# Hybrid decoder trunk on one Trainium2 core: the head norms' widening copy moved ahead of a wait, waits of the side jobs changed, the embedding gate's tanhs issued together

## The chip, the core and the metric

The kernel runs on one core of one Trainium2 chip. The metric is the device time of one execution in microseconds (us), from the first to the last instruction with what the launch adds around them. Engines are named as the profile names them: PE is TensorE (PEld its weight loads), DVE VectorE, ACT ScalarE, POOL GpSimd, SP SyncE, which here does nothing but issue the transfers of weights and small tables from HBM.

## The reference, cut to what matters

256 tokens of width 1024 go through two layers. In each, one projection `w_in` of the normed tokens feeds four mixers (SSD, native sparse attention or NSA, RWKV-7, sliding-window attention or SWA), whose gated outputs are summed and added to the tokens; then comes a feed-forward part (dense in layer 0, two of eight experts in layer 1) and a gated per-layer embedding:

```
x = x + W_o( sum_m sigmoid(gate_m(h)) * (mixer_m(u_m) @ P_m) )
x = x + FFN(RMSNorm(x))
x = x + sigmoid(x @ W_pg) * (p[i] @ W_pp)
# inside RWKV-7, H = 8 heads of N = 64:
kk = (k * k_k).reshape(B, S, H, N)
kk = kk / max(sqrt(sum(kk * kk, -1)), 1e-12)          # head norm 1
o  = (o - mean) * rsqrt(var + RWKV_GN_EPS)            # head norm 2, also over 64
o  = o + sum(r * k * r_k, -1) * v                     # "bonus"
```

The SWA mixer rotates its queries and keys by the tokens' positions (rope), with tables of cosines and sines over 256 positions.

## The kernel before, in words

**Units.** All products with weights go through one list of units, one panel of 128 x 1024 (or 128 x 832) weights each. A unit of kind `fm` is 24 matmuls of 128x256, three for each of eight slices of the width; one of kind `tokm` has 12 or 24 wider ones. Every fp32 product is three matmuls (`mm3`, L357 to L359): high part by high part, low by high, high by low.

**A unit's way.** SP fetches the panel (`raw`, L264) into one of four buffers. ACT copies the high part `H` (L313), and the low part `L = raw - H` is made by DVE for the first three quarters of the columns (L316) and by POOL for the rest (L318). There are three pairs of `H` and `L`. A raw buffer comes free when all three engines have read it, and SP issues its transfers in order. PE needs `H` and the DVE part of `L` from the unit's first slices on, and POOL's quarter only in its later slices.

**Side jobs.** The mixers' other work (norms, scans, attention) is written as generators, which run between pieces of the units: each piece calls `tick()`, which takes 0.64 off the time that every job has left, and a job whose time is up emits its instructions up to the next `yield`. The number after `yield` gives the wait, rounded up to whole ticks, unless the table `WAITS` names another number of ticks for this yield of this job. So the table sets how many of the units' matmuls stand on PE between an instruction of a side job and the one that depends on it. In an `fm` unit one tick is six matmuls. Every engine takes its instructions strictly in the emitted order. When a unit needs a flag of a side job, ticks go by without units until the flag is set.

**The jobs that matter here.** `rwkv_half` runs four times (two halves of the heads in each layer; `rwkv_half0` and `1` are layer 0). For each head norm it calls `head_rsqrt`: four tiny matmuls sum the squares per head (`ssp`, L708), DVE takes a reciprocal root in small steps (`rsqrt_steps`, the last writes `ssc`, L412), and then the job waits 1.8, which is three ticks. After that `head_spread` widens the 8 columns `ssc` to 512 (`wide`, a DVE copy, L717), and PE transposes `wide` (`spr`, L721) so that DVE can multiply by it (`kkn`, L765, or `cen`, L913). Later in the job DVE makes `bq` (L787), and PE sums it over the heads (`bop`, L792), then come `gram` (L818) and `tok` (L800) products. The last step of a half sets a flag that the first NSA unit (`open_pool`) needs. The job `swa` takes the projected queries from ACT (`rraw`, L1363) and PE rotates them (`rotp`, L1380); DVE, POOL and ACT make the rotated, split query of it (`rtmp`, `qTH`).

**Rope tables.** In layer 0 a job issues a transfer of the positions on SP (`pos`, L391), and POOL converts them and reduces the angles in ten instructions (L520 to L530). They stand in POOL's order between two quarters of weight panels.

**Embedding.** `ple_units` handles the gate's columns in two halves. For each of two token tiles ACT takes a tanh (`th`, L1619), DVE adds and multiplies (L1620 on), and squares for the next norm follow.

Of the kernel before, what the change touches and what calls it, by code (L numbers as in the profile page):

```python
# [15 lines left out]
ALU = mybir.AluOpType  # L16
# [32 lines left out]
def _consts():  # L49
# [37 lines left out]
    for k, v in cols.items():  # L87
# [27 lines left out]
}  # L115


def trunk_kernel(tc, I, out, dbg=None, upto=99):
    nc = tc.nc
# [24 lines left out]
    x = big.tile([P, 2, D], F32, name="x")  # L144
# [25 lines left out]
    def K(name):  # L170
        o, w = COFF[name]
        return cst[:, o:o + w] if o < NC32 else cstb[:, o - NC32:o - NC32 + w]
# [16 lines left out]
    def psb(name="psb"):  # L189
        return psB.tile([P, 512], F32, tag="b", name=name)  # L190
# [7 lines left out]
    def unit(run, pieces=None, nk=0, ncol=0, need=None, spawn=None, rich=None, ahead=True, lend=False):  # L198
        stream.append((run, pieces, nk, ncol, need, spawn, rich, ahead, lend))
# [18 lines left out]
    def tick(t=0.64):  # L218

        for g in list(side):  # L220
            g[1] -= t
            if g[1] > 1e-3:
                continue
            if len(g) == 2:
                nm = g[0].gi_code.co_name
                c = spawned[nm] = spawned.get(nm, -1) + 1
                g += [nm + str(c), 0]
                w = wait_of(g, 0)
                if w > 1e-3:
                    g[1] = w - t  # L230
                    if g[1] > 1e-3:
                        continue
            try:
                d = next(g[0])
                if d == "poll":
                    g[1] = 0.3
                else:
                    g[3] += 1
                    g[1] = wait_of(g, d or 1.2)
            except StopIteration:  # L240
                side.remove(g)
# [172 lines left out]
    def rsqrt_steps(t):  # L414
        w = 2 if t.free_size() == 1 else 3
        for n, _ in enumerate(rsqrt_ops(t)):
            if n in (2, 2 + w, 2 + 2 * w):
                yield 0.64
# [5 lines left out]
    def squares(i, n):  # L424

        act(junk, x[:, i, n * 512:n * 512 + 512], AF.Square, accum_out=ssq[:, n, i:i + 1])  # L426
        if n == 0:
            ts(ssq[:, 0, i:i + 1], ssq[:, 0, i:i + 1], 1.0 / D, EPS, ALU.mult, ALU.add)
# [76 lines left out]
    def cols_of(src, c0, w):  # L505
        r = src.rearrange("(k p) n -> p k n", p=P)
        return lambda v, k0, nk: [(v, r[:, k0:k0 + nk, c0:c0 + w])]
# [32 lines left out]
    gfin = []  # L540
# [6 lines left out]
    def mixing(l, after):  # L547
# [105 lines left out]
        def R(name):  # L653
            return Z.mxr.tile([P, 512], F32, tag="r2", name=name, bufs=R2)
# [48 lines left out]
        def head_rsqrt(sq, c, op):  # L703

            ps = psb("ssp")
            bo = K("bo")[:, 0:P:64]
            for n in range(4):
                mm(ps[:, 2 * n:2 * n + 2], sq[:, n * P:(n + 1) * P], bo, start=True, stop=True)  # L708
            ss = Z.mxr.tile([P, 4, 2], F32, tag="ssc", name="ssc", bufs=2)
            ts(ss, ps[:, 0:8].rearrange("p (n h) -> p n h", h=2), c, None, op)  # L710
            yield from rsqrt_steps(ss)
            yield 1.8
            return ss

        def head_spread(ss):
            wide = R("wide")
            vec.tensor_copy(wide.rearrange("p (n v) -> p n v", v=64),  # L717
                            ss.rearrange("p n h -> p (n h)").unsqueeze(2).to_broadcast([P, 8, 64]))
            ps = psb("spr")
            for n in range(4):  # L720
                nc.tensor.transpose(ps[:, n * P:(n + 1) * P], wide[:, n * P:(n + 1) * P], ident)  # L721
            return ps
# [855 lines left out]
    def ple_units(l, Z):  # L1578
        unit(lambda: l + 1 in early and early[l + 1]())

        def settle():
            while side:
                tick()
            rich_close(f"ffn{l}")

        unit(settle)
        if Z.before is not None:
            unit(Z.before)

        def begin():  # L1590
            Z.late = Z.ctx.enter_context(tc.tile_pool(name=f"late{l}", bufs=1))
            rich_open(f"ple{l}", 2, 3)
            if last and upto >= 20:
                for i in range(2):
                    for n in range(2):
                        fin[i, n] = Z.late.tile([P, 512], F32, tag=f"fin{i}{n}", name="fin")
            if Z.after is None:
                Z.xT = to_T(x, 8, big, "hT", name="xT")
                return
            steps = []  # L1600
            Z.xT = to_T(x, 8, big, "hT", name="xT", steps=steps)
            Z.after()
            steps.pop(0)()
            steps.pop(0)()

            def rest():
                for f in steps:
                    f()
                    yield 0.64
                flags.add(f"xT{l}")  # L1610
            side.append([rest(), 0.0])

        unit(begin)
        last = l + 1 == DEPTH
        fin = {}

        def add(i, n, ps):
            th = Z.late.tile([P, 512], F32, tag="th", name="th", bufs=2)
            act(th, ps, AF.Tanh, scale=0.5)  # L1619
            stt(th, th, 1.0, Z.pj[:, i, n * 512:n * 512 + 512], ALU.add, ALU.mult)  # L1620
            o = x[:, i, n * 512:n * 512 + 512]
            stt(o, th, 0.5, o, ALU.mult, ALU.add)  # L1622
            squares(i, n)
            if last and upto >= 20:
                nc.gpsimd.tensor_tensor(fin[i, n], o, gfin[n], ALU.mult)

        def first_half(psl):
            for i in range(2):
                add(i, 0, psl[i])

        def second_half(i, ps):
            add(i, 1, ps)
            if not last and i:
                rms((0, 1), True)
            if last and upto >= 20:
                rms((i,), False)
                for n in range(2):
                    o, r = fin[i, n], rs[0][:, i:i + 1]
                    if n or i == 0:
                        ts(o, o, r, None, ALU.mult)  # L1640
                    else:
                        act(o, o, AF.Copy, scale=r)  # L1642
                    nc.sync.dma_start(out[0, i * P:(i + 1) * P, n * 512:n * 512 + 512], o)

        for n in range(2):
            tok_matmul(lambda: Z.xT, 8, 512, cols_of(I["ple_gate"][l], n * 512, 512), second_half if n else first_half,
                       rich=f"ple{l}", by_token=n == 1, half_need=[f"xT{l}"] if Z.after is not None and n == 0 else None)
        unit(lambda: rich_close(f"ple{l}"))
        unit(Z.ctx.close)
# [55 lines left out]
    def rich_open(key, nraw, nspl):  # L1705

        c = ExitStack()
        r = c.enter_context(tc.tile_pool(name="r" + key, bufs=nraw))
        w = c.enter_context(tc.tile_pool(name="w" + key, bufs=nspl))
        rich[key] = Slots(r, nraw, w, nspl)  # L1710
        rich[key].close = c.close

    def rich_close(key):
        rich.pop(key).close()
# [254 lines left out]
    for l in range(DEPTH):  # L1969
        if upto <= 10 * l:  # L1970
            break
        Z = SimpleNamespace(ctx=ExitStack(), GT={}, OHT={}, rc={}, before=None, after=None)
        mixing(l, (lambda l=l, Z=Z: ffn_open(l, Z), lambda Z=Z: ple_turn(Z),
                   lambda n, l=l, Z=Z: (moe_settled if l % 2 else dense_settled)(l, Z, n)))
        dump_x(f"xmix{l}")
        if upto <= 10 * l + 1:
            break
        (moe if l % 2 else dense)(l, Z)
# [29 lines left out]
```

## Time and profile before

| what | value |
|---|---|
| median of three timed runs | 2025.96 us (2024.52 to 2027.46) |
| the profiled execution | 2029.14 us, span of its instructions 2027.3 us |
| busy: PE / DVE / ACT / POOL | 1941.3 / 1535.2 / 1176.2 / 1108.8 us |
| mean granted TensorE clock | 0.987 of full speed |

PE is busy for 96% of the span, so a reader looks for its idle stretches and for stretches in which its clock is not full. All durations in the rows below come from the profiled execution, and times of day are us from its first instruction. A row of the timeline with `[3.30 <-DVE wide L717]` says that the engine stood idle for 3.30 us just before, and that the DVE instruction of line 717 ended the wait.

### The profile page before, as it was taken

The page shows a single profiled execution, that of the slowest core. Times are in us where ns is not written, and L with a number is a line of the kernel's source. Part 1 is how long each engine was busy: PE and PEld are TensorE (multiplying, and loading weights), DVE is VectorE, ACT ScalarE, POOL GpSimd, SP SyncE. Part 2 cuts the span into 40 slices and gives each one's busy share as a digit, 9 for nine tenths or more (in the row PEclk, how much of TensorE's full clock was granted, in tenths as well). Part 3 has the DMA queues.
Part 4 walks back from the last instruction along what each step waited for, and adds up shares of the span by engine and source line. Part 5 has one row for each costly group of instructions (what it writes and reads, how often), then busy time and mean ns, then how long its engine had stood idle before and what let it go on. Part 6 is the DMA issues. An engine that isn't in the chain of part 4 may idle for free. (4 is left out here: it accounts for less than half of the span.)

```text
span 2027.3 us, 37453 instructions
## 1 busy us (share of the span) xinstructions
PE 1941.3 (96%) x13236; PEld 1612.7 (80%) x13236; DVE 1535.2 (76%) x2432; ACT 1176.2 (58%) x1786; POOL 1108.8 (55%) x976
## 2 busy tenths in 40 slices
PE   6999999999999899999999999999999999999996
PEld 6898787778999688878877777787777777877775
DVE  5565656656554656656666589999999999999995
ACT  5434345455444433334454568777877787778773
POOL 4533254555554353424444566676867666768673
PEclk9999999999999999999999999999999999999998
DMA  7322464466665443227344889899999999999972
GB/s 199 96 75 88 106 142 135 125 173 198 190 189 150 120 120 85 86 82 155 107 135 135 283 275 356 306 327 344 358 349 325 344 360 349 325 347 359 347 254 96
DMA packets 419441, 435.78 MB, mean 215 GB/s; under 512 B 67876, under 2 KB 355624, under 8 KB 419240
## 3 DMA queue, kind: packets, MB, share of 16 engines
q1 hardware_dynamic: 419240, 433.26, 68.1%
q8 instruction: 106, 1.74, 0.3%
q14 instruction: 95, 0.78, 0.1%
HBM read 432.13 MB, written 1.05 MB: 214 GB/s over the span
## 5 line engine op out<-in xcount | busy, mean ns | idle before, releaser
L318 POOL TENSOR_TENSOR L<-raw,H 128x256 fp32r<-128x256 f32 (+1 forms) x794 | 941.9, 1195 | 835.5 <-ACT H L313 658.1
L316 DVE TENSOR_TENSOR L<-raw,H 128x768 fp32r<-128x768 f32 (+1 forms) x792 | 935.2, 1210 | 193.4 <-ACT H L313 186.8
L313 ACT CAST H<-raw 128x1024 fp32r<-128x1024 f32 x794 | 828.2, 1047 | 268.0 <-PE tokm L359 60.8
L357 PE MATMUL gu<-H,GH 128*128 128x512 f32 x704 | 286.4, 407 | 0.1
L358 PE MATMUL gu<-L,GH 128*128 128x512 f32 x704 | 278.9, 396 | 0.5 <-DVE L L316 0.5
L359 PE MATMUL gu<-H,GL 128*128 128x512 f32 x704 | 278.2, 395 | 1.1 <-DVE GL L370 1.1
L359 PE MATMUL dn<-H,aL 128*128 128x512 f32 x440 | 174.7, 397 | 1.4 <-DVE aL L367 1.4
L357 PE MATMUL dn<-H,aH 128*128 128x512 f32 x440 | 174.8, 397 | 1.2 <-ACT aH L366 1.0
L358 PE MATMUL dn<-L,aH 128*128 128x512 f32 x440 | 174.9, 398 | 0.0
L357 PE MATMUL fm<-hTH,H 128*128 128x256 f32 x560 | 168.1, 300 | 0.0
L358 PEld LDWEIGHTS gu<-L,GH 128*128 128x128 f32 x704 | 132.6, 188 | 37.3 <-DVE L L316 10.8
L358 PE MATMUL fm<-hTL,H 128*128 128x256 f32 x560 | 159.1, 284 | 0.0
L359 PE MATMUL fm<-hTH,L 128*128 128x256 f32 x560 | 158.9, 284 | 0.0
L359 PEld LDWEIGHTS gu<-H,GL 128*128 128x128 f32 x704 | 132.3, 188 | 30.3 <-DVE GL L370 2.7
L357 PEld LDWEIGHTS gu<-H,GH 128*128 128x128 f32 x704 | 132.3, 188 | 27.1 <-ACT GH L369 0.5
L357 PE MATMUL tokm<-H,hTH 128*128 128x512 f32 (+1 forms) x320 | 136.9, 428 | 0.0
L358 PE MATMUL tokm<-L,hTH 128*128 128x512 f32 (+1 forms) x320 | 125.5, 392 | 0.5 <-DVE L L316 0.5
L359 PE MATMUL tokm<-H,hTL 128*128 128x512 f32 (+1 forms) x320 | 125.6, 392 | 0.0
L357 PEld LDWEIGHTS fm<-hTH,H 128*128 128x128 f32 x560 | 107.6, 192 | 5.7 <-issue 2.7
L358 PEld LDWEIGHTS fm<-hTL,H 128*128 128x128 f32 x560 | 107.7, 192 | 0.3
L359 PEld LDWEIGHTS fm<-hTH,L 128*128 128x128 f32 x560 | 107.6, 192 | 0.0
L358 PEld LDWEIGHTS dn<-L,aH 128*128 128x128 f32 x440 | 82.9, 188 | 23.1 <-DVE L L316 6.3
(500 smaller groups left out, 3518.0 us busy)
## 6 DMA issues: line engine op xcount, KB each, us to landing
raw<-moe_w_gate SPq DMA_DIRECT2D x341, 256.0 KB
raw<-moe_w_up SPq DMA_DIRECT2D x341, 256.0 KB
raw<-moe_w_down SPq DMA_DIRECT2D x169, 512.0 KB
raw<-w_in SPq DMA_DIRECT2D x126, 512.0 KB
raw<-ffn_w_gate SPq DMA_DIRECT2D x22, 512.0 KB
raw<-ffn_w_up SPq DMA_DIRECT2D x22, 512.0 KB
raw<-ffn_w_down SPq DMA_DIRECT2D x22, 512.0 KB
raw<-w_in SPq DMA_DIRECT2D x32, 256.0 KB
```

The costliest lines, as they stand in the source:

```text
L313: nc.scalar.copy(H[:, :n], raw[:, :n])
L316: tt(L[:, :m], raw[:, :m], H[:, :m], ALU.subtract)
L318: nc.gpsimd.tensor_tensor(L[:, m:n], raw[:, m:n], H[:, m:n], ALU.subtract)
L357: mm(o, l[0], r[0], start=start, stop=False)
L358: mm(o, l[0], r[1], start=False, stop=False)
L359: mm(o, l[1], r[0], start=False, stop=stop)
```

## The change

Three edits. The widening copy is put into `head_rsqrt`, before the wait, and that wait's own default goes from 1.8 to 2.4 (four ticks). `WAITS` gives longer waits: after `ssc` and `wide` of the first norm (yield 6 of each half) 5 or 6 ticks for 2 or 3, between `bq` and the job's next look at its flag (yield 10 of halves 0 and 2) 4 or 5 for 2, after the second norm's copy (yield 43) 4 or 6 for 2 or 3, and before three of the SWA rotations 7 to 9 for 4. In the embedding's first half both tanhs are issued before the additions, and the squares after both.

```diff
-    'rwkv_half0': {1: 7, 3: 2, 6: 2, 12: 1, 15: 3, 18: 2, 20: 5, 22: 2, 23: 4, 24: 2, 28: 7, 29: 1, 31: 4,
-        32: 5, 33: 6, 34: 4, 35: 4, 39: 3, 41: 5, 42: 3, 43: 2, 44: 2},
+    'rwkv_half0': {1: 7, 3: 2, 6: 5, 10: 4, 12: 1, 15: 3, 18: 2, 20: 5, 22: 2, 23: 4, 24: 2, 28: 7, 29: 1, 31: 4,
+        32: 5, 33: 6, 34: 4, 35: 4, 39: 3, 41: 5, 42: 3, 43: 4, 44: 2},
...
-    'swa0': {2: 6, 3: 2, 5: 5, 6: 7, 11: 3, 13: 6, 14: 3},
+    'swa0': {2: 6, 3: 2, 4: 9, 5: 5, 6: 7, 11: 3, 13: 6, 14: 3},
...
             yield from rsqrt_steps(ss)
-            yield 1.8
-            return ss
-
-        def head_spread(ss):
             wide = R("wide")
             vec.tensor_copy(wide.rearrange("p (n v) -> p n v", v=64),
                             ss.rearrange("p n h -> p (n h)").unsqueeze(2).to_broadcast([P, 8, 64]))
+            yield 2.4
+            return wide
+
+        def head_spread(wide):
             ps = psb("spr")
...
         def first_half(psl):
+            ths = [gate(ps) for ps in psl]
             for i in range(2):
-                add(i, 0, psl[i])
+                add(i, 0, ths[i])
+            for i in range(2):
+                settled(i, 0)
```

On DVE, at the first head norm of layer 0, the difference (- before, + after) reads as follows; `r` and `v` are parts of the RWKV projection, `L` the low part of a weight panel.

```order
 L412 SCALAR_TENSOR_TENSOR ssc<-rsa,rsy 128x8
+L713 COPY wide<-ssc 128x512
 L668 SCALAR_TENSOR_TENSOR r<-fm,par,r 128x255
 L316 TENSOR_TENSOR L<-raw,H 128x640
-L717 COPY wide<-ssc 128x512
+L668 SCALAR_TENSOR_TENSOR v<-fm,par,v 128x255
 L765 SCALAR_TENSOR_TENSOR kkn<-k,par,spr 128x256 x2
```

The copy now stands right behind `ssc`. On PE `spr` moves 18 `fm` matmuls back, from 36 behind `ssp` to 54 behind it, so that `kkn` comes after a further projection step on DVE; `bop` moves 15 `tokm` matmuls back.

On PE, in the value units of layer 0 some microseconds later, the rows around the second slice of the third such unit stood like this before (the numbers tell tiles apart; `H_636` and `L_637` are that unit's parts, `kap`, `beta` and `v` belong to the RWKV job).

```order
L358 MATMUL tokm_643<-L_637,hTH_175 128x416
L359 MATMUL tokm_643<-H_636,hTL_176 128x416
L800 MATMUL tok_757<-cst_82,kap_598 64x64 x16
L800 MATMUL tok_776<-cst_82,v_580 64x64 x16
L357 MATMUL tokm_643<-H_636,hTH_175 128x416
L358 MATMUL tokm_643<-L_637,hTH_175 128x416
```

And with the change (the unit's parts are now `H_633` and `L_634`):

```order
L358 MATMUL tokm_640<-L_634,hTH_175 128x416
L359 MATMUL tokm_640<-H_633,hTL_176 128x416
L818 MATMUL gram_705<-AR_598,beta_601 64x128 x8
L357 MATMUL tokm_640<-H_633,hTH_175 128x416
L358 MATMUL tokm_640<-L_634,hTH_175 128x416
L359 MATMUL tokm_640<-H_633,hTL_176 128x416
L800 MATMUL tok_719<-cst_82,beta_601 64x64 x16
L818 MATMUL gram_738<-AR_598,kap_618 64x128 x8
```

Five groups of the RWKV job that stood ahead of this slice (one `tok` of `beta`, two `gram` of `kap`, one `tok` of `kap`, one of `v`) now stand behind it. The slice is the first of its unit that reads POOL's quarter.

On POOL, from the product `kp` of the first RWKV half to the first instruction of the rope tables, the difference is two rows that change places; the quarter of the third value unit still stands behind the ten rope instructions, as before.

```order
 L770 TENSOR_TENSOR kp<-kp,k 128x512
-L776 TENSOR_TENSOR AR<-r,Dd 128x8x64
-L318 TENSOR_TENSOR L<-raw,H 128x192
+L318 TENSOR_TENSOR L<-raw,H 128x192
+L776 TENSOR_TENSOR AR<-r,Dd 128x8x64
 L782 TENSOR_TENSOR kap<-kp,inv 128x512
 L520 CAST scr<-pos 128x256
```

The quarter of the second value unit is now ahead of `AR`. In the emission itself, the second RWKV half of each layer now ends three ticks later, and in each layer three ticks go by without units ahead of `open_pool`, where none did before.

## Rows read from the trace of the kernel before

**Rows 1.** The page's first part: engines, busy us, share, instructions.

```profile
PE 1941.3 (96%) x13236; PEld 1612.7 (80%) x13236; DVE 1535.2 (76%) x2432; ACT 1176.2 (58%) x1786; POOL 1108.8 (55%) x976
```

**Rows 2.** PE's waits, whole span: us in total, times, longest us.

```profile
PE spr L721 <- DVE wide L717: 16.4, 8, 3.3
...
PE rotp L1380 <- ACT rraw L1363: 6.4, 3, 2.6
...
PE bop L792 <- DVE bq L787: 3.0, 2, 2.0
```

**Rows 3.** PE's waits in 720 to 740 us, early in layer 1.

```profile
PE spr L721 <- DVE wide L717: 2.1, 1, 2.1
PE bop L792 <- DVE bq L787: 2.0, 1, 2.0
```

**Rows 4.** PE's waits in 780 to 990 us, the rest of layer 1's mixers.

```profile
PE spr L721 <- DVE wide L717: 5.5, 3, 2.5
PE rotp L1380 <- ACT rraw L1363: 3.8, 2, 2.2
```

**Rows 5.** DVE's timeline at the first head norm: start, duration, instruction.

```profile
38.46 0.17 DVE L412 SCALAR_TENSOR_TENSOR ssc<-rsa,rsy 128x8 f32<-128x8 f32 x1
...
38.94 0.81 DVE L316 TENSOR_TENSOR L<-raw,H 128x640 fp32r<-128x640 f32 x1
39.67 0.42 DVE L717 COPY wide<-ssc 128x512 f32<-128x512 f32 x1
```

**Rows 6.** PE's timeline at the same place.

```profile
36.66 0.28 PE L359 MATMUL fm<-hTH,L 128*128 128x256 f32 x1
40.23 0.63 PE L721 MATMUL spr<-cst,wide 128*128 128x128 f32 x4 [3.30 <-DVE wide L717]
```

**Rows 7.** Windows: stretch, length, busy PE, PEld, DVE, ACT, POOL, PEclk, DMA.

```profile
40.80:44.20 3.40, 3.40 (x18) 3.40 (x17) 2.72 (x6) 0.00 (x0) 1.70 (x1) 0.50 0.58 159
...
989.70:993.10 3.40, 3.14 (x7) 2.49 (x8) 2.26 (x7) 2.24 (x7) 2.13 (x2) 0.51 0.00 0
...
44.20:47.60 3.40, 3.40 (x29) 3.39 (x29) 2.25 (x3) 1.45 (x3) 3.40 (x4) 0.99 0.01 2
...
696.00:703.00 7.00, 2.96 (x14) 2.44 (x14) 5.28 (x25) 4.27 (x10) 0.00 (x0) 0.51 0.00 0
```

**Rows 8.** POOL's timeline around the start of the rope tables.

```profile
44.73 1.19 POOL L776 TENSOR_TENSOR AR<-r,Dd 128x512 f32<-128x512 f32 x1
45.89 1.22 POOL L318 TENSOR_TENSOR L<-raw,H 128x192 fp32r<-128x192 f32 x1
...
51.76 0.40 POOL L520 CAST scr<-pos 128x256 f32<-128x256 int32 x1 [2.95 <-DMA pos<-positions]
...
59.84 2.75 POOL L318 TENSOR_TENSOR L<-raw,H 128x192 fp32r<-128x192 f32 x3
```

**Rows 9.** SP's queue: the issue of the positions' transfer.

```profile
47.56 0.57 SPq L391 DMA_DIRECT2D pos<-positions  x1
```

**Rows 10.** PE's timeline in layer 0's value units.

```profile
54.74 1.15 PE L800 MATMUL tok<-cst,beta 64*64 64x64 f32 x32
55.72 1.04 PE L818 MATMUL gram<-AR,kap 64*64 64x128 f32 x16
...
62.69 0.35 PE L358 MATMUL tokm<-L,hTH 128*128 128x416 f32 x1
```

**Rows 11.** ACT's timeline behind layer 0's rotation.

```profile
303.66 1.04 ACT L313 CAST H<-raw 128x1024 fp32r<-128x1024 f32 x1
```

**Rows 12.** PE's timeline there, where that panel is used.

```profile
305.75 0.50 PE L358 MATMUL tokm<-L,hTH 128*128 128x512 f32 x1 [0.29 <-DVE L L316]
```

**Rows 13.** ACT's timeline behind layer 1's last waited-for rotation.

```profile
989.79 1.05 ACT L313 CAST H<-raw 128x1024 fp32r<-128x1024 f32 x1
```

**Rows 14.** PE's timeline there, where that panel is first used.

```profile
997.99 0.48 PE L357 MATMUL tokm<-H,hTH 128*128 128x512 f32 x1
```

**Rows 15.** ACT's timeline, first half of layer 0's embedding gate.

```profile
684.83 0.59 ACT L1619 ACTIVATE th<-tokm 128x512 f32<-128x512 f32 x1
```

More of the change, by code (lines that the diff above doesn't have):

```diff
@@ L1615, in ple_units, with gate, add @@
         fin = {}
-        def add(i, n, ps):
+        def gate(ps):
             th = Z.late.tile([P, 512], F32, tag="th", name="th", bufs=2)
             act(th, ps, AF.Tanh, scale=0.5)
+            return th
+        def add(i, n, th):
             stt(th, th, 1.0, Z.pj[:, i, n * 512:n * 512 + 512], ALU.add, ALU.mult)
@@ L1622, in add, with settled @@
             stt(o, th, 0.5, o, ALU.mult, ALU.add)
+        def settled(i, n):
             squares(i, n)
             if last and upto >= 20:
-                nc.gpsimd.tensor_tensor(fin[i, n], o, gfin[n], ALU.mult)
+                nc.gpsimd.tensor_tensor(fin[i, n], x[:, i, n * 512:n * 512 + 512], gfin[n], ALU.mult)
         def first_half(psl):
+            ths = [gate(ps) for ps in psl]
             for i in range(2):
-                add(i, 0, psl[i])
+                add(i, 0, ths[i])
+            for i in range(2):
+                settled(i, 0)
         def second_half(i, ps):
-            add(i, 1, ps)
+            add(i, 1, gate(ps))
+            settled(i, 1)
             if not last and i:
```

10 rows, old and new, of the table WAITS are left out of this document.

## The prediction, made before the changed kernel ran

> **What bounds the kernel now.** I read the page first: PE is busy for 96% of the span [rows 1], so nothing that shortens DVE, ACT or POOL counts by itself. What counts is PE's idle time and its clock. The list of PE's waits by line comes next. The waits that this change touches stand together in it: eight for `wide`, 16.4 us, three of `rotp`, 6.4, two of `bop`, 3.0, in sum 25.8 us [rows 2]. Cut by windows, layer 1 holds 2.1 + 5.5 of `spr`, 2.0 of `bop` and 3.8 of `rotp` [rows 3, 4]. So layer 0 holds 16.4 - 7.6 = 8.8 of `spr` (3.3 of them at the first norm [rows 6]), 1.0 of `bop` and 2.6 of `rotp`.
>
> Then the clock. Behind seven of these stalls lies a stretch of 3.4 us in which the granted clock is 0.50 or 0.51, the lower level (1.2 GHz); the first and the last of the seven are shown [rows 7]. Three are in layer 0 (the first behind the 3.3 us stall), four in layer 1. In the first PE does 18 matmuls, in the equally long stretch right behind it, at full clock and with like matmuls, 29: (1 - 18/29) x 3.4 = 1.3 us lost. In the last PE itself is busy for only 3.14 us, so less is lost. I take 1.1 for each, 7.7 in all; the bounds are 0 and 1.7 (half of 3.4).
>
> **The copy and the first longer wait.** At the first norm `ssc` ends at 38.46 + 0.17 = 38.63 and `wide` only at 40.09, because a projection step and the 0.81 us subtraction stand between them on DVE [rows 5]. PE is there from 36.94 and waits 3.30 [rows 6]. With the change the copy ends at 38.63 + 0.42 = 39.05, and `spr` stands 18 matmuls later on PE, at 3.4/29 = 0.117 us each 2.1 us, at 36.9 + 2.1 = 39.0. The wait vanishes. The other seven are 2.5 us at most [rows 2, 4], get as many or more ticks, and lose the instructions between `ssc` and the copy too: I take all eight as gone where they stand. `bop` (2.0 and 1.0) and `rotp` (2.2 at most in layer 1) move by 15 `tokm` matmuls and by several ticks, which covers them as well.
>
> A wait of PE that goes is only a gain if what PE does next is ready. So I go through the places.
>
> **Layer 0, first norm and `bop`: 3.3 + 1.0 + 1.3 = 5.6, given back.** In the second slice of the third value unit (the low part's matmul at 62.69 [rows 10]) PE needs POOL's quarter. It is made behind the ten rope instructions, the first of three quarters from 59.84; shared by columns (192 of 640 in 2.75 us) it is done at 60.67 [rows 8], 2 us before it is used. The change takes five groups of about 0.98 us (55.72 - 54.74 [rows 10]) from ahead of this slice, 4.9 us. Without any recovered time PE would come at 62.69 - 4.9 = 57.8, with it at 52.2. POOL's part hangs on the transfer of the positions: POOL waits 2.95 us for it and starts at 51.76 [rows 8]. It is issued at 47.56 [rows 9], behind a panel's transfer, whose buffer comes free when POOL's quarter of the second value unit ends, at 45.89 + 1.22 = 47.11 [rows 8]. With the change that quarter is ahead of `AR` (1.19 [rows 8]), and all of it follows a `wide` that ends 1.04 earlier: at most 2.2 us earlier, at least, if POOL's share is not what holds it or the transfer lands among other panels, 0. I take 1.6, nearer to the upper end, as both rows point that way. The part is ready at 60.67 - 1.6 = 59.1. PE, there at 52.2, waits 6.9 us in one piece: against 57.8 this is 1.3 us lost (0 to 2.9), and the 5.6 are gone.
>
> I expect the lower clock behind a wait of that length, and for longer than behind the short ones: from 696 to 703 us, where PE was busy for only 2.96 of 7.0 us, it stood at 0.51 throughout [rows 7]. At most 3.5 is lost by that, at least the 1.3 of a short one; I take 1.7, nearer to the short one, as PE was idle in much of that long row. This place gives -3.0.
>
> The Trainium skill, page "SBUF — State Buffer", section "Who interferes with whom", states that a DVE instruction with two SBUF inputs contends with a GpSimd instruction that reads SBUF, and that the later one is held fully. The quarter of 192 columns took 1.22 us beside DVE [rows 8], against 0.83 in the run of three: the row is slower, as the rule has it. Moved ahead of `AR`, the quarter meets DVE's subtraction (0.81 [rows 5]); by the rule the chain would be held by up to 0.8, and the whole sum below would be 0.8 less.
>
> **Layer 0, the other three norms: 8.8 - 3.3 = 5.5, and two half-clock stretches, 2.2.** These 7.7 stay, less one thing: the second half of RWKV now ends three ticks later, and three ticks pass without units ahead of `open_pool`. A tick is worth 6 x 0.117 = 0.7 us. The bounds are 0 (PE goes on with side work) and 2.1; I take 2.1, as DVE's last steps of RWKV and its split of the next panels stand in one queue. Left: 5.6.
>
> **Layer 0, rotation: 2.6, not gained.** The next panel is copied by ACT from 303.66 to 304.70 [rows 11], and PE already waits 0.29 us for its low part at 305.75 [rows 12]. ACT's and DVE's order up to that copy hangs on the scores before it, not on this `rotp`. PE would come 2.6 us sooner and wait there. Gain 0 (at most 2.6).
>
> **Layer 1.** First norm and `bop`: 2.1 + 2.0 and two half-clock stretches, 6.3; there are no rope tables here. The other three norms: 5.5 + 1.1 - 2.1 for the three ticks, 4.5. Rotation: 3.8 + 1.1 = 4.9; here the panels are early: one that ACT has done at 990.84 [rows 13] is first used at 997.99 [rows 14], so PE can run 7 us ahead before it waits.
>
> **Embedding.** The first half's tanh starts [rows 15] while PE goes on with the second half's matmuls, which cover it, the additions and the squares. If that cover were gone, the second tanh's 0.59 us would be what the order is worth; only the second half, whose order is unchanged, ends the part. I take 0.
>
> **Sum.** I subtract 1.5 for small new waits that a changed order brings (estimate: two of the size of a short `bop` wait, with something over for the split's lag; bounds 0 and 5). -3.0 + 5.6 + 0 + 6.3 + 4.5 + 4.9 - 1.5 = 16.8 us. The profiled execution took 2029.1, 3.2 above the median of the timed runs; 2029.1 - 16.8 = 2012.3, and on the runs' scale 2025.96 - 16.8 = 2009.2. I say 2009.
>
> **The rivals.** *Everything is kept.* POOL's chain and the rotation's panel come earlier with the rest, and the empty ticks cost nothing: 25.8 + 7.7 = 33.5, 1992.5; 1992 to 2003 with one part missing. For it: POOL waits for a transfer, not for work [rows 8]. Against it: the third quarter would have to come 8 us earlier, and nothing in the rows moves it by over 2.2. Chance 0.15.
>
> *Mostly given back.* Layer 1's norms return as waits for panels too, as DVE (76% of the whole span [rows 1]) is the real limit around them. Layer 0's -3.0 and layer 1's 4.9 + 4.5 remain, 6 to 8: 2015 to 2022. Against it: the 7 us lead of [rows 13, 14]. Chance 0.2.
>
> *The change does nothing that can be measured.* All stalls come back one unit later, with the lower clock behind them: within 4 us of before, 2022 to 2030. Chance 0.08.
>
> *Slower.* The panels' split on DVE sets the pace of the mixer stages. Then every removed wait returns at the next panel with its clock loss, and the rope stall (-3.0), the empty ticks of both layers (-4.2) and 1.5 come on top: 2026 + 8.7 = 2034.7. It decides itself where panels are less than the removed 2 us ahead of PE; layer 0's rotation is such a place [rows 12], layer 1's is not. Chance 0.05.
>
> **Numbers.** My forecast, 2003 to 2015 around 2009, has 0.52. The 8 in 10 range takes most of the first two rivals in: 1996 to 2019. A measurement of this kernel can tell about 0.2%, 4 us, from no change. Faster: 0.52 + 0.15 + 0.2 = 0.87; same 0.08; slower 0.05.
>
> **What would show it.** The list of PE's waits has no or almost no `spr`, `bop` and `rotp`. In their place stands one wait of 6 to 8 us of `tokm` on POOL's `L` at 51 to 60 us, with the clock at the lower level behind it, and one of about 2 us on a panel behind layer 0's rotation. The seven half-clock stretches are gone. The first embedding half lasts as long as before. I am wrong if POOL's quarter is ready when PE comes, if waits on `L` or `H` appear in layer 1 around 740, 930 or 990 us, or if the three empty ticks show as idle PE ahead of `open_pool`.

## The result, and the profile after

The changed kernel takes 2042.14 us (median of 5 runs, 2036.98 to 2042.94), the kernel before 2027.46 (5 runs): ratio 1.0073, 95% interval 1.0056 to 1.0090. It is about 15 us slower, where 2009 us was forecast. The profiled execution has a span of 2040.3 us, 13.0 more than before. Executions of one and the same kernel differ by some us, the longer ones mostly at a lower mean granted clock (in the experiments the kernel before took 2021.7 to 2029.8 us, at 0.991 to 0.986), so times are compared by medians, and the waits of a single profiled execution are read with that in mind.

PE's waits, whole span of the changed kernel (us in total, times, longest):

```profile
PE trp L463 <- ACT xs L452: 10.8, 3, 6.8
PE bop L792 <- DVE bq L787: 10.1, 4, 2.7
...
PE tokm L358 <- POOL L L318: 4.4, 2, 3.9
...
PE m L807 <- POOL LO L833: 3.6, 3, 1.9
PE rhs L869 <- DVE St L891: 3.6, 2, 2.1
PE tokm L357 <- ACT H L313: 3.3, 2, 2.8
```

Of the three waits that were to go [rows 2], `spr` has gone (16.4 us before; 0.2 is left) and `rotp` too (6.4), but `bop` has grown from 3.0 to 10.1. In their place stand waits that the trace of before hardly had: of the RWKV job's next steps (`m` on `LO`, `rhs` on `St`), on POOL's quarter and on a panel's `H`.

To see how much was lost where, take the stretch from the first projection matmul of a layer to the same matmul of the unit list in every kernel (number 1248 of the layer's `fm` and `tokm` matmuls), some 345 us. Windows of the kernel before (the layer 0 stretch, then layer 1; columns as in [rows 7]):

```profile
15.00:360.00 345.00, 330.62 (x3462) 287.49 (x3460) 216.68 (x478) 148.79 (x293) 152.76 (x145) 0.99 0.44 115
703.30:1047.40 344.10, 329.75 (x3459) 287.05 (x3457) 216.61 (x469) 145.72 (x290) 144.62 (x132) 0.98 0.40 107
```

And of the changed kernel:

```profile
15.00:373.80 358.80, 340.40 (x3460) 293.54 (x3458) 221.13 (x478) 148.12 (x293) 156.63 (x145) 0.96 0.41 111
714.90:1061.50 346.60, 331.28 (x3461) 285.75 (x3459) 214.12 (x469) 144.87 (x290) 146.16 (x132) 0.99 0.40 106
```

In layer 0 the same work takes 13.8 us longer: PE is idle for 18.4 us instead of 14.4, and busy for 9.8 us more with as many matmuls, because its mean granted clock falls from 0.99 to 0.96. In layer 1 it takes 2.5 longer, where a gain of 15.7 was forecast. Both together are 16.3; the rest of the span gives 3.3 back. PE's waits in this stretch of layer 1, in the changed kernel:

```profile
PE bop L792 <- DVE bq L787: 5.3, 2, 2.7
PE rhs L869 <- DVE St L891: 2.1, 1, 2.1
PE m L807 <- POOL LO L833: 1.7, 2, 0.9
PE sc L357 <- ACT Pm L1140: 1.3, 1, 1.3
PE tokm L358 <- DVE L L316: 1.0, 2, 0.5
```

Before, 13.4 us of `spr`, `rotp` and `bop` stood here, and 1.0 us of other waits. Now `bop` has 5.3, and eleven small waits have 10.0 (`sc` are products of the attention scores).

The places of the prediction in the changed kernel. DVE's timeline at the first norm, which answers to [rows 5], and PE's, to [rows 6]:

```profile
38.36 0.17 DVE L412 SCALAR_TENSOR_TENSOR ssc<-rsa,rsy 128x8 f32<-128x8 f32 x1
38.56 0.43 DVE L713 COPY wide<-ssc 128x512 f32<-128x512 f32 x1
```

```profile
38.65 0.28 PE L359 MATMUL fm<-hTH,L 128*128 128x256 f32 x1
39.13 0.63 PE L721 MATMUL spr<-cst,wide 128*128 128x128 f32 x4 [0.20 <-DVE wide L713]
...
49.49 1.12 PE L792 MATMUL bop<-bq,cst 128*128 128x512 f32 x2 [2.19 <-DVE bq L787]
...
59.84 0.72 PE L358 MATMUL tokm<-L,hTH 128*128 128x416 f32 x1 [3.90 <-POOL L L318]
```

The 3.3 us at `spr` are gone. 10 us later PE waits 2.19 for `bq` (1.04 before), and at the third value unit 3.90 for POOL's quarter. SP's and POOL's rows of the positions, to [rows 8, 9]:

```profile
46.47 0.57 SPq L391 DMA_DIRECT2D pos<-positions  x1
```

```profile
50.57 0.40 POOL L520 CAST scr<-pos 128x256 f32<-128x256 int32 x1 [1.42 <-DMA pos<-positions]
...
59.19 1.83 POOL L318 TENSOR_TENSOR L<-raw,H 128x192 fp32r<-128x192 f32 x3
```

The transfer is issued 1.1 us earlier, POOL starts 1.2 earlier, its quarter 0.65 earlier. Windows of the changed kernel, in this order: around the end of this wait, behind the wait on `H` at the rotation, and behind `bop`:

```profile
57.70:64.50 6.80, 4.66 (x51) 3.85 (x51) 0.00 (x0) 0.58 (x1) 3.24 (x5) 0.50 0.53 135
317.10:323.90 6.80, 6.52 (x18) 4.63 (x19) 4.80 (x9) 3.00 (x8) 4.98 (x4) 0.50 0.39 108
50.90:54.30 3.40, 3.40 (x20) 2.75 (x16) 1.20 (x3) 0.65 (x1) 3.05 (x5) 0.50 0.00 0
```

In these three places the lower clock stands behind a new wait, and two of the stretches are twice as long as the seven of the prediction.

### The profile page after: what moved, and what is told of

Same layout as the page of the kernel before. It is cut to its first block, busy times and chain, and to the rows that moved or that the text cites. A ratio compares the mean times of both kernels' runs of the same rounds, so it can differ in the third digit from the quotient of the medians.

```text
span 2040.3 us, 37469 instructions
## 1 busy us (share of the span) xinstructions
PE 1951.2 (96%) x13236; PEld 1617.2 (79%) x13236; DVE 1536.1 (75%) x2432; ACT 1174.6 (58%) x1786; POOL 1122.0 (55%) x976
## 5 line engine op out<-in xcount | busy, mean ns | idle before, releaser
L318 POOL TENSOR_TENSOR L<-raw,H 128x256 fp32r<-128x256 f32 (+1 forms) x794 | 954.2, 1211 | 844.8 <-ACT H L313 688.6
L358 PE MATMUL gu<-L,GH 128*128 128x512 f32 x704 | 278.5, 396 | 0.5 <-DVE L L316 0.5
L358 PE MATMUL dn<-L,aH 128*128 128x512 f32 x440 | 174.1, 396 | 0.0
L358 PEld LDWEIGHTS gu<-L,GH 128*128 128x128 f32 x704 | 132.6, 188 | 36.5 <-DVE L L316 10.1
L358 PE MATMUL fm<-hTL,H 128*128 128x256 f32 x560 | 158.8, 284 | 0.0
L358 PE MATMUL tokm<-L,hTH 128*128 128x512 f32 (+1 forms) x320 | 127.6, 399 | 5.5 <-POOL L L318 4.4
L358 PEld LDWEIGHTS fm<-hTL,H 128*128 128x128 f32 x560 | 107.7, 192 | 0.2
L358 PEld LDWEIGHTS dn<-L,aH 128*128 128x128 f32 x440 | 82.6, 188 | 21.8 <-DVE L L316 4.9
```

The source lines that it names most:

```text
L318: nc.gpsimd.tensor_tensor(L[:, m:n], raw[:, m:n], H[:, m:n], ALU.subtract)
L358: mm(o, l[0], r[1], start=False, stop=False)
```

## The experiments

Every kernel is set against the kernel before on the same chip; ratios have their 95% interval in brackets, and 0.001 is 2.0 us.

**First: the parts by themselves.** The theory was that the longer RWKV waits do the harm; the rivals were the earlier copy itself and the SWA waits. The first kernel has the copy alone, with the ticks of before:

```diff
+            wide = R("wide")
+            vec.tensor_copy(wide...)
             yield 1.8
-            return ss
+            return wide
```

> The copy alone, behind ssc, with the ticks of before. Theory T (the longer RWKV waits do the harm, because they put the job's instructions behind others in the queues of DVE and POOL): the spr waits fall from 16.4 us to about 4 (2.1 at the first norm of layer 0, 1.6 in layer 1), half of the gain stays, 2013 to 2020 us. Rival C (the earlier copy itself makes DVE's and POOL's work meet, as bq at 2.80 us in the changed kernel against 1.18 before): no gain or a loss, 2027 to 2033, and bq over 2 us.

Measured 2013.48 us, 0.9936 (0.9922 to 0.9950). The second has the new `rwkv_half` rows of `WAITS` alone, with the copy behind the wait:

> The RWKV waits of the change alone, the copy behind the wait as before. Theory T: nearly the whole loss is here, 2036 to 2042 us, with bop waits of about 10 us and a wait of tokm on POOL's L of 3 to 5 us. Rival C: under half of the loss, 2027 to 2033.

Measured 2047.5 us, 1.0109 (1.0091 to 1.0126). The third has the two `swa` rows alone:

> The SWA waits alone. Theory T: rotp waits go (6.4 us), layer 0 gets a wait on H of 2.8 us in their place, layer 1 keeps some 4: 2021 to 2027 us. Rival S (the SWA waits do a good part of the harm, as the changed kernel shows 6.8 us at half clock behind the wait on H): 2030 to 2034.

Measured 2025.25, 0.9996 (0.9985 to 1.0006): 6.4 us of `rotp` gone, 3.3 us on `H` in their place, and in layer 1 also waits of `sc` on ACT (1.3 and 0.8) and of `tokm` on DVE's `L` (1.0). The fourth has the embedding's order alone:

> The order of the embedding's tanhs alone. Both theories: no change, 2025 to 2029 us.

Measured 2024.59, 0.9988 (0.9979 to 0.9997): a gain of some 2 us, 0.6 to 4.3 by the interval.

So the copy gains 13 us and the RWKV ticks lose 22. Already these don't add up: 13 and 22 make a loss of 9, and the whole change loses 15; on top of the ticks, the copy and the two other parts gain only 7 (1.0109 to 1.0073). The profile of the copy alone, PE's waits of the whole span, and the windows of the same two stretches:

```profile
PE spr L721 <- DVE wide L713: 5.0, 4, 2.7
...
PE bop L792 <- DVE bq L787: 4.0, 2, 2.4
```

```profile
15.10:351.50 336.40, 326.91 (x3461) 284.52 (x3460) 217.78 (x478) 148.82 (x294) 153.88 (x145) 0.99 0.46 119
695.10:1028.00 332.90, 323.68 (x3461) 282.48 (x3460) 216.28 (x469) 145.60 (x290) 145.84 (x132) 1.00 0.44 111
```

The copy brings the result of a DVE chain to PE earlier, and leaves PE's own order alone. Idle time falls to 9.5 and 9.2 us, and busy time by 3.7 and 6.1, since the clock hardly drops any more: of the seven half-clock stretches one is left, behind the 2.7 us of `spr` at the first norm. The two stretches are 8.6 + 11.2 = 19.8 us shorter, the whole span 18.5. By the medians the gain is 13 (the profiled executions took 2010.64 us, where the median is 2013.48, and 2029.14, where it is 2025.96), so part of the 19.8 is the difference of two executions. With the ticks alone (second kernel) the waits are:

```profile
PE spr L721 <- DVE wide L717: 10.2, 8, 2.0
PE bop L792 <- DVE bq L787: 10.1, 4, 2.6
...
PE tokm L358 <- POOL L L318: 5.0, 1, 5.0
```

The ticks take 6.2 us off `spr`, and `bop` alone takes back 7.1.

**Second: which of the ticks.** On top of the early copy, one row of yields at a time:

```diff
# yield 6 (behind the first norm's copy), halves 0 to 3
-6: 2   (3)   2   (3)
+6: 5    6    5    6
# yield 43 (second norm), or yield 10 (bq to bop), in the same way
-43: 2  (3)   2   (3)        -10: (2)  (2)  (2)  (2)
+43: 4   6    4    6         +10:  4   (2)   5   (2)
```

> The early copy, and of the longer waits only those behind the first norm's copy (yield 6: 5, 6, 5, 6 ticks). Theory T6 (this move puts bq, the products of the RWKV job and POOL's steps later in the queues, behind panels of the next unit): most of the loss of the longer waits returns, 2026 to 2034 us, with bop waits of 7 us or more and the wait on POOL's L. Rival T10/T43 (the loss is in the other two waits): 2011 to 2018.

> The early copy, and only the longer waits behind the second norm's copy (yield 43: 4, 6, 4, 6 ticks). Theory T6: little, 2011 to 2017 us against 2013.5 of the copy alone. Rival T43 (the job's later end, with three ticks without units ahead of the NSA part, is what costs): 2020 to 2028.

> The early copy, and only the longer waits between bq and bop (yield 10: 4 and 5 ticks, halves 0 and 2). Theory T6: the bop waits fall from 4.0 us to under 1, but in layer 0 the products move behind the slice that needs POOL's quarter, so a wait there of 1 to 4 us: 2010 to 2018 us. Rival T10 (this move brings the wait on POOL's L with a long half-clock stretch): 2018 to 2026.

Yield 6: 2031.12, 1.0018 (1.0008 to 1.0027), some 17 us more than the copy alone, with 14.3 us of `bop`. Yield 43: 2012.13, 0.9931 (0.9917 to 0.9944), nothing lost. This kernel does not test the three empty ticks that its rival names: in its emission none go by ahead of `open_pool`; yield 6 alone brings none either, while the changed kernel, with both, has them. Yield 10: 2024.8, 0.9997 (0.9988 to 1.0006), 12 us more, where the theory had at most some 5: `bop` does fall to 2.0, but waits on POOL's quarter (2.4), on `LO` (4.1 and 2.5) and on `X` (3.1) come behind it.

**Third: POOL's quarter.** The changed kernel with the value units' low part wholly on DVE:

```diff
-m = n - n * pool_part // 16 // 32 * 32 if ns else 0
+m = n if n == 832 else n - n * pool_part // 16 // 32 * 32 if ns else 0
```

> The changed kernel, but the value units' low parts wholly on DVE (no quarter on POOL), so that PE doesn't wait for POOL behind the rope instructions. If that wait of 3.9 us and the half-clock stretches around it (10 us) are a large part of the loss: 6 to 9 us less than the changed kernel, 2033 to 2036. If PE then waits for the next late thing instead (bq or LO): 2039 to 2043.

Measured 2035.13, 1.0045 (1.0032 to 1.0059): about 6 us less than the changed kernel, and the wait on POOL's quarter is gone. This wait and its half-clock stretches are worth some 6 of the 28 us (1.0073 - 0.9936) that lie between the early copy alone and the whole change.

**Fourth: first or second halves, one tick, a farther `bop`.** Yield 6 at 6 ticks for the second halves alone, and at 3 for the first halves alone, both on the early copy; and the changed kernel with 8 ticks between `bq` and `bop` in all halves:

> The early copy, and the longer wait at yield 6 for the second halves alone (3 to 6 ticks), where the copy alone leaves no wait of spr. Theory Q (each half loses by itself, as bq gets behind a panel's split and the SSD convolution in DVE's queue): half of the 17.6 us of all four, 2020 to 2025 us, bop waits of about 6 us. Rival F (the loss is in the first halves, beside the rope tables and the value units): 2012 to 2016.

> The early copy, and one tick more at yield 6 in the first halves (3 for 2), where the copy alone still leaves 2.7 and 1.8 us of spr. If a tick only moves PE's step: the spr waits fall to 2.0 and 1.1 or less, 2009 to 2013 us. If already one tick puts bq later in the queue: bop up by 1 us or more each, 2013 to 2019.

> The changed kernel with 8 ticks between bq and bop in all four halves, so that the bop waits (10.1 us) go. If they are the cost: 2026 to 2033 us. If the job's delay passes on to the next step (LO, the scan, the units behind it): 2036 to 2046.

The second halves alone: 2031.6, 1.0027 (1.0018 to 1.0036), as much as all four, though `bop` waits only 6.8 us here; 5.9 of `sap` on `rh` and 3.1 of `m` on `LO` stand further down the job. One tick in the first halves: 2027.22, 1.0005 (0.9997 to 1.0014), 14 us more than without it; `spr` falls as expected, to 3.2, and `bop` rises to 7.3, `m` on `LO` to 4.0. I had expected the loss to divide among the halves and to grow with the number of ticks; both expectations failed. The farther `bop`: 2037.6, 1.0059 (1.0046 to 1.0072), 3 us less than the changed kernel, which the two intervals leave open. `bop` doesn't wait any more, but PE then waits 11.0 us in one piece for POOL's quarter, and 6.6 for `LO`:

```profile
PE tokm L352 <- POOL L L312: 11.5, 2, 11.0
...
PE m L801 <- POOL LO L827: 6.6, 2, 3.3
```

(the table has fewer lines there, so L352 is L358 of the others).

**Fifth: contention with POOL, or the queue.** In the changed kernel DVE's forerunners of `bop` are slow. DVE's lines of the changed kernel (count, busy us, mean ns), and before these were 555, 1009 and 954 ns:

```profile
L787 DVE SCALAR_TENSOR_TENSOR bq<-r,par,kp 128x256 f32<-128x256 f32 x8 | 7.2, 932 | 0.0
L780 DVE SCALAR_TENSOR_TENSOR beta<-beta,kkn 128x512 f32<-128x512 f32 x4 | 6.0, 1494 | 0.0
L778 DVE SCALAR_TENSOR_TENSOR beta<-ta,inv 128x512 f32<-128x512 f32 x4 | 4.8, 1203 | 0.0
```

So the three products of the job on POOL (L770, L776, L782) were put on DVE, in the changed kernel and, as a control, in the early copy alone; and, on the early copy, a tick was taken away from yield 6 of the second halves (its diff is not shown):

```diff
-nc.gpsimd.tensor_tensor(kp, kp, kt, ALU.mult)
+tt(kp, kp, kt, ALU.mult)          # and so for AR's second half and kap
```

> The changed kernel with the three products of the RWKV job that POOL makes (kp, AR's second half, kap) on DVE, so that DVE's bq and beta meet no POOL product. Theory P (bq and its forerunners on DVE are slow, 932 and 1494 ns against 555 and 1009 before, because POOL works beside them, and this is what makes bop wait): bq back to about 450 ns, bop waits from 10.1 us to under 6, 2032 to 2038 us. Rival Q (only the place in the queues counts): three more instructions of 0.7 us each in DVE's queue, bop waits of 12 us or more, 2041 to 2050.

> The control: the early copy alone, with the same three products on DVE. Theory P: bop waits from 4.0 us to about the same or less, 2008 to 2016. Rival Q: 2 us more of DVE's queue per half, 2016 to 2024.

> The early copy, and one tick less at yield 6 in the second halves (2 for 3), where the early copy leaves no wait of spr. If the job's steps only have to come early: spr there may wait 0.5 us, 2008 to 2014. If every tick's move changes which work meets on DVE and POOL, in either direction, as the one tick of the first halves did (13.7 us more): 2018 to 2030.

The changed kernel: 2036.49, 1.0051 (1.0039 to 1.0063). The control: 2008.7, 0.9912 (0.9899 to 0.9925). Both are 4 to 5 us better, and `bq` takes 594 and 473 ns on DVE:

```profile
L787 DVE SCALAR_TENSOR_TENSOR bq<-r,par,kp 128x256 f32<-128x256 f32 x8 | 3.5, 473 | 0.0
```

(the control). So DVE's products are slower beside POOL's, but moving POOL's away gains about the same with and without the change: the two kernels still lie 28 us apart (1.0051 - 0.9912), so this doesn't explain the difference; the changed kernel still has 7.9 us of `bop`. One tick less: 2016.77, 0.9957 (0.9945 to 0.9970), 4 us worse than the copy alone. The old count of three was the better one, but a move in this direction is cheap.

**Sixth: the place of `bq`.** DVE's timeline of the changed kernel in the second half of layer 0:

```profile
116.25 1.52 DVE L960 SCALAR_TENSOR_TENSOR cacc<-fm,hw,cacc 128x253 f32<-128x253 f32 x3 [1.07 <-ACT cacc L957]
118.32 0.42 DVE L963 SCALAR_TENSOR_TENSOR xbc<-cth,cacc 128x256 f32<-128x256 f32 x1 [0.55 <-ACT cth L962]
119.26 0.96 DVE L316 TENSOR_TENSOR L<-raw,H 128x768 fp32r<-128x768 f32 x1 [0.52 <-ACT H L313]
120.13 1.34 DVE L787 SCALAR_TENSOR_TENSOR bq<-r,par,kp 128x256 f32<-128x256 f32 x2
```

With the copy alone the same instructions stand like this:

```profile
106.64 0.87 DVE L787 SCALAR_TENSOR_TENSOR bq<-r,par,kp 128x256 f32<-128x256 f32 x2
108.44 1.52 DVE L960 SCALAR_TENSOR_TENSOR cacc<-fm,hw,cacc 128x253 f32<-128x253 f32 x3 [0.93 <-ACT cacc L957]
```

The ticks have moved `bq` behind the SSD convolution of the next unit and behind the next panel's split, and both wait for ACT (0.52 to 1.07 us each), so `bq` comes late though DVE had time before. PE's `bop` waited 2.61 for it:

```profile
121.62 0.67 PE L792 MATMUL bop<-bq,cst 128*128 128x512 f32 x1 [2.61 <-DVE bq L787]
```

In layer 1's second half the order is the same, with `bq` at 810.33. The changed kernel with `bq` emitted one wait earlier, and nothing else moved:

```diff
+            bq = R("bq")
+            ...                     # the two products of bq
             yield 2.4
-            bq = R("bq")
-            ...
             yield 1.0
```

> The changed kernel with bq emitted one wait earlier, right behind beta, so that on DVE it isn't queued behind the next panel's split and the SSD convolution; nothing else moves. Theory Q (bop waits because bq stands behind work of the units in DVE's queue): bop from 10.1 us to under 5, 2031 to 2037 us. Rival (the delay passes on to the next step of the job): 2038 to 2043, with the sum of PE's waits in the mixers as before.

Measured 2034.32, 1.0037 (1.0023 to 1.0051), 7 us less than the changed kernel. `bop` is down to 1.9 us, so most of its wait was the place of `bq` in DVE's queue. But waits behind it have grown:

```profile
PE tokm L358 <- POOL L L318: 7.6, 2, 7.2
```

(4.4 and 3.9 before this edit), and `m` on `X` from 1.3 to 3.5: of 8.2 us that `bop` loses, 5.4 return at these two. PE now comes sooner to a quarter of POOL's that is ready no sooner (the matmul that needs it starts at 59.91, and at 59.84 before this edit).

**Last: a version that beats both.** The early copy, yield 43, SWA waits of layer 1 only, and the embedding's order; then with POOL's three products on DVE; then with the early `bq` too:

> The parts that cost nothing by themselves, together: the early copy, the longer waits at yield 43, the SWA waits of layer 1, the embedding's order; the waits at yields 6 and 10 and layer 0's SWA as before. If the parts add up, 1 to 5 us below the copy with yield 43 (2012.1), 2006 to 2011 us, with rotp waits in layer 0 alone. If layer 1's rotation wait moves to a panel as in layer 0: 2011 to 2014.

> The best parts (early copy, yield 43, layer 1's SWA, the embedding's order: 2010.0) with the three POOL products on DVE, which gave 4.8 us over the early copy alone. If this adds up: 2003 to 2007 us. If both take the same waits: 2007 to 2010.

> The same with bq one wait earlier. If the bop waits of the first halves (some 3 us with their half-clock stretches) are bq's place in the queue: 1999 to 2004 us. If not: within 2 us of the kernel without it.

Measured 2009.99, 0.9924 (0.9911 to 0.9937); 2008.8, 0.9916 (0.9903 to 0.9930); 2007.32, 0.9913 (0.9899 to 0.9927). The parts don't add up: over the early copy alone (2013.48) the last gains some 5 us, and with the control of the fifth group (2008.7, copy and POOL's products alone) it is the same within its interval.

## Why the prediction was wrong, point by point

**The copy** was right: by itself it gains 13 us, with `spr` down from 16.4 to 5.0.

**The ticks** are the step that failed: "`bop` (2.0 and 1.0) and `rotp` (2.2 at most in layer 1) move by 15 `tokm` matmuls and by several ticks, which covers them as well." I asked of each removed wait whether the next panel would be ready, and not where the moved job's next instructions would stand in DVE's and POOL's queues. `bop`, booked as 3.0 us gained, went from 3.0 to 10.1, and two halves wait for it that did not before. In the second halves `bq` had fallen behind steps that wait for ACT (shown by the queue and by the kernel that moves `bq` alone). At yield 6 and at yield 10 each, the ticks cost 17 and 12 us over the early copy. The longer waits moved PE's waits to the job's next steps: take `bop`'s away, and two thirds of it return at POOL's quarter and at `X`.

**The 1.5 for small new waits** (bounds 0 to 5) was the second term that failed. Besides `bop`, POOL's quarter and the 2.8 on `H`, the trace of before hardly had these: in layer 0 `m` on `LO` 1.9, `rhs` on `St` 1.4, and three more of 2.0 in sum; in layer 1 some 9 us. In all it is about 14 us.

**The half-clock stretches** were to go, 7.7 us gained. With the copy alone six of the seven are gone. In the changed kernel layer 0 spends 9.8 us more of PE's busy time on the same matmuls, the largest part of its loss. Low stretches stand there behind waits for `bop`, POOL's quarter, `m`, `rhs` and `H`, so the sign of this term hung on the terms above.

**POOL's quarter in layer 0** was right as a mechanism, and too large by itself: 3.9 us of wait instead of 6.9, because `bop`'s wait and a half-clock stretch ahead of it kept PE from coming at 52.2 (it came at 55.94); with `bop`'s wait cut it was 7.16. POOL's part came 0.65 us earlier, where I took 1.6: `kp` started only 0.49 earlier and took 3.02 us for 2.27, and one of the ten rope instructions took 1.44 for 0.85. The quarter itself is 0.61 us and not the 0.83 shared out by columns, for the 2.75 of the run in [rows 8] are 0.61, 0.60 and 1.50, the last one beside DVE's subtraction. The quarter moved ahead of `AR` took 1.03 us, not longer than the 1.22 before. (The bounds of the loss against 57.8 should have begun at 0.7, not at 0: 60.67 - 2.2 is 58.5.) The whole place is worth about 6 us (third experiment).

**Layer 0's rotation** was right: the wait moved to the panel's `H`, 2.83 us, and the SWA rows by themselves change nothing. A half-clock stretch came with it that the wait of 2.61 before did not have; the kernel with the SWA rows alone has it too (0.50 from 306.0 to 309.4).

**Layer 1** was wrong by 18 us (15.7 gained, 2.5 lost): its panels were early, as I had read [rows 13, 14] (waits for `L` and `H` are 1.9 us of its list), but `bop` has 5.3 us for 2.0, and the small waits of the term above take the rest of what had gone. The rotation's 4.9 were not gained: in the kernel with the SWA rows alone, the 3.8 of `rotp` are gone and 3.5 have come, 2.1 of `sc` on ACT and 1.4 for panels.

**The three empty ticks** (2.1 us per layer) show no idle time of PE in the changed kernel. PE goes from the half's last product (`gp`) straight on to the next unit; layer 0, and layer 1 is alike (948.25 and 948.93):

```profile
257.62 1.03 PE L920 MATMUL gp<-lor,gup 128*128 128x256 f32 x4
258.29 0.47 PE L357 MATMUL fm<-hTH,H 128*128 128x256 f32 x1
```

No kernel has these ticks taken out alone, so that they cost nothing elsewhere is not shown. **The embedding**, booked at 0, gained some 2 us by itself.

**The rival "slower"** had the right sign with the wrong mechanism: it let the panels set the pace; by the list of waits, what set it were mostly the RWKV job's own steps.

**Open** is why one tick in two halves (14 us), three in the two others (18) and three in all (17) cost about the same. That the RWKV ticks cause the loss is shown; of how they do it, the place of `bq` and POOL's quarter are shown in part (7 and 6 us of the 28), and contention with POOL is ruled out as the difference. The runs don't tell which of the job's later steps (`LO`, `X`, `St`) carries the rest, how much of it is clock, nor whether a new table of waits for them would regain it.

## What to carry to other kernels

Here a wait of the bounding engine was shortened to good effect where its cause came earlier; giving the engine more to do ahead of it mostly moved the wait to the next link of the same chain. So follow every later link through the queues of the engines it passes before booking the gain. In a schedule by counted waits, one changed count moves everything behind it: test each edit of such a table alone, for here one part gained 13 us, another lost 22, and the rest gained some 2. And where the clock falls behind a stall, the stall costs more than its length: layer 0 of the changed kernel lost 4.0 us to idle time and 9.8 to slower matmuls.

## What the runs showed of the hardware that was not expected

DVE's products grew by up to twice their length beside POOL's: `bq` of 128x256 took 473 ns with POOL's products taken away, 555 in the kernel before and 932 in the changed one; `beta` of 128x512 (L780) took 788 ns in the control, 1009 before and 1494 in the changed kernel. The Trainium skill, page "SBUF — State Buffer", section "Who interferes with whom", has it that a DVE instruction with two SBUF inputs contends with a GpSimd instruction that reads SBUF; these rows agree. Moving the three products off POOL was worth 4 to 5 us of the whole here.

The clock didn't follow a wait's length alone. At layer 0's rotation it stayed at full speed behind a wait of 2.61 us before the change (a row of PE's timeline, then a window):

```profile
301.73 0.70 PE L1380 MATMUL rotp<-rraw,cst 128*128 128x256 f32 x2 [2.61 <-ACT rraw L1363]
...
301.80:305.20 3.40, 3.40 (x15) 2.67 (x15) 2.26 (x6) 1.64 (x3) 0.36 (x1) 1.00 0.00 0
```

In the kernel with the RWKV ticks alone, the same instruction after as long a wait stands in a half-clock stretch:

```profile
311.94 1.22 PE L1380 MATMUL rotp<-rraw,cst 128*128 128x256 f32 x2 [2.62 <-ACT rraw L1363]
...
311.40:314.80 3.40, 2.86 (x7) 2.29 (x8) 2.13 (x7) 1.73 (x5) 0.00 (x0) 0.53 0.00 0
```

And in the changed kernel, behind a wait of 2.83 at the same place, it stood at 0.50 for 6.8 us:

```profile
317.19 0.79 PE L357 MATMUL tokm<-H,hTH 128*128 128x512 f32 x1 [2.83 <-ACT H L313]
```

So a stall's price could not be told from its length, in this case.
